# A gated mixer and ConvFFN step on one core: recurrence products moved from GpSimd to VectorE, one operand's low parts formed on VectorE, raw weight blocks of the gate pairs placed in other buffers

## The chip, the cores and the metric

The kernel runs on one NeuronCore of a Trainium2 chip. The metric is device time in microseconds of one execution, the median of several runs. Five engines matter here: TensorE (PE, the matmuls; PEld is its weight load), VectorE (DVE), ScalarE (ACT), GpSimd (POOL) and SyncE (SP), which here only issues DMA transfers. They run side by side and wait for one another through semaphores.

## The reference, cut to what matters

One layer is computed for 512 grid tokens of a denoising step and, with the same weights, for 128 context tokens; the kernel treats them as 640 columns. All is float32. In short:

```python
h = rmsnorm(x, norm1_g) * (1 + sc1) + sh1            # sc, sh, g from silu(c) @ w_ada + b_ada
proj = h @ w_in                                      # 13 sections
y_b = hgrn2_bidir(b_q, b_ff, b_fb, b_i, b_g, ...)    # recurrence, forward and backward
merged = sum_i sigmoid(h @ w_gate_i + b_i) * (y_i @ w_br_i)   # i = a, b, c, d
x = x + g1 * (merged @ w_o)
h = rmsnorm(x, norm2_g) * (1 + sc2) + sh2
x = x + g2 * conv_ffn(h, w_up, cw, cb, w_down)
```

The recurrence of a head is, with gates f = lb + (1 - lb) sigmoid(z), keys k = (1 - lb) sigmoid(-z) and decays that are products of f between two positions: `scores[t, s] = sum_d q[t, d] k[s, d] decay[t, s, d]`, `o = scores @ v` plus the part that comes from the carried state, once forward and once backward.

## The kernel before, in words

**Precision and products.** Each float32 matmul is made from three products of a high part (rounded to fp32r by a ScalarE copy) and a low part (the rest, by a VectorE subtraction): high x high, high x low, low x high. So each weight block costs a ScalarE copy and a VectorE subtraction (`feat`, L354 and L355, L367 and L368 in the `wsplit` and `prep` helpers), and each activation operand as well. In some places the subtraction is replaced by `low_dma`: ScalarE writes the negated high part, and a transfer issued by GpSimd adds the raw block onto it in SBUF.

**Order of the work.** The program is a list of units (a weight tile each): 26 projection tiles, 8 gate tiles of branch d, the gate pairs, 8 tiles of w_o, the up projection, 22 tiles of w_down. `ahead` loads the blocks of the next four units (SP) and splits those of the next two. Beside the units run generators (`hgrn`, `gmlp`, `conva`, `attn`, `ada_cols`, `norm2`), each of which yields the time after which it wants to go on, in microseconds of a planner's clock. `tick` and `pe` advance this clock by the estimated PE time of each matmul group, and `tick` starts the generators that are due; `drain` steps them all until a condition holds. This fixes the order in which instructions are written down. The framework then orders each engine's instructions itself, except those issued through `Ordered` (`ovec`, `oact`, `opool`) while `fixed[0]` is set, in the gate pairs and in the up pairs. [...]

**Recurrence** (`hgrn`). The state is not scanned; instead the scores are built in seven levels l = 0..6 with blocks of B = 2^l positions. At level l PE multiplies the queries `qq` with the keys of the neighbouring block (L559); VectorE or ScalarE puts the result into the score tile (L565, L569); then four multiplies in place (`ups`, L579) extend keys `kk` and queries `qq` by the gates `ff`, and L583 extends the gates. The matmul takes one tile of keys, half of whose columns are backward and half forward keys: `keys(l + 1)` builds it after the second multiply, half on GpSimd (L530), half on ScalarE (L531). Ahead of the levels come the sum `ksum` (L493), its product with the queries (L509), and the products of neighbours, one half on GpSimd and one on VectorE (L515, by the table `NE`). `along` sums over features by a matmul (L503). PE meanwhile works through the projection tiles; the section `i` is evacuated by ScalarE in L949.

**Gain columns** (`ada_cols`). 24 columns of w_ada are multiplied with silu(c) on VectorE (L256, two products per column) while the recurrence runs, 8 more (40 to 47) during the first half of w_down. Every eighth column of a gain ends with `gain_rows`, a PE transpose (L283), a ScalarE copy (L286) and a store.

**Gate pairs** (`g_pair`). Two gate tiles (n and n + 4 of a branch) are made with seven instead of eight block products. A pair has two raw blocks of 128x10x128; `gp_load` takes one from the pool `raw` (three buffers) and the other from `raw` too for even pairs, from the region `G` for odd ones. Pair 0 is loaded while the last branch-d gate tiles run (`gate_tile`, sigmoid L986); `g_a`, `g_sums`, `g_b`, `g_c` split blocks and their sums. The region G holds attention's values before the pairs and a part of x after them.

**Up projection** (`up_all`, `up_pair`). It uses the same seven products per pair, with seven activation operands made by `operands(c0, c1)`: x6 in region A, x5 in B, x7 in D; first for columns 0 to 192, then, when the last token tile is normalised, for 192 to 320. Their low parts: x6 by VectorE, x5 by transfer for the first columns and by VectorE for the last, x7 by transfer both times. For the first four pairs two of the seven products are made ahead (`up_start`), and the rest in 22 pairs. Much of this goes through `Ordered`, so the profile gives line L132 for it.

Of the kernel before, what the change touches and what calls it, by code (L numbers as in the profile page):

```python
# [9 lines left out]
F32 = mybir.dt.float32  # L10
# [3 lines left out]
ALU = mybir.AluOpType  # L14
AX = mybir.AxisListType

P = 128
HD = [4, 5, 2.1, 7, 2.2, 1.4, 1.5, 5, 2.0, 2, 11]
NE = [lambda p, v: p, lambda p, v: v]
OUTS = 1  # L20
NPAIR = 22
BRIDGE = 4
# [29 lines left out]
def tile_step(ctx: ExitStack, tc: tile.TileContext, a: dict, outs: list, dbg=None):  # L52
# [7 lines left out]
    rp = ctx.enter_context(tc.tile_pool(name="rp", bufs=3))  # L60
# [46 lines left out]
    def nm(s):  # L107
        cnt[0] += 1
        return f"{s}_{cnt[0]}"

    def region(tag, shape, dt=F32):
        return big.tile(shape, dt, tag=tag, name=nm(tag))
# [23 lines left out]
    ten, vec, pool, act, mm = nc.tensor, nc.vector, nc.gpsimd, nc.scalar.activation, nc.tensor.matmul  # L136
# [97 lines left out]
    def ada_cols(fs, tag, homes, gap):  # L234

        cr = region(tag, [P, 2, D])
        cf = cr.rearrange("p v c -> p (v c)")
        nc.sync.dma_start(cf, a["cc"].rearrange("v c -> (v c)").partition_broadcast(P))
        act(cf, cf, AF.Silu)
        raws = {}  # L240

        def load(f):
            if f in fs and f not in raws:
                raws[f] = homes(f)
                nc.sync.dma_start(raws[f], a["w_adt"][f - 16])

        load(fs[0])
        yield HD[4]
        for f in fs:
            load(f + 1)  # L250
            raw = raws.pop(f)
            junk = gp.tile([P, D], mybir.dt.bfloat16, tag="gt", name=nm("junk"))
            ar = sp.tile([P, 2], F32, tag="red", name=nm("ar"))
            for v in range(2):
                tc.keep_in_program_order(
                    vec.scalar_tensor_tensor(raw if v else junk, raw, 1.0, cr[:, v], ALU.mult, ALU.mult,  # L256
                                             accum_out=ar[:, v:v + 1]))
                yield HD[5]
            if f // 8 in (2, 5):
                vec.tensor_scalar(gcol[:, f // 8 // 5, :, f % 8], ar, p1[:, C_BADA + f:C_BADA + f + 1],  # L260
                                  None, ALU.add)
                if f % 8 == 7:
                    yield 2
                    gain_rows(f // 8 // 5)
            else:
                modulate(f, ar)
            yield gap
            while "hgrn_out" in R and "hgrn_done" not in R:
                yield 1
        R["ada%d" % fs[-1]] = True  # L270
# [213 lines left out]
    def hgrn():  # L484
        ff, kk, hd = R["FF"], R["KK"], R["HD"]
# [3 lines left out]
        sq = hd[:, 0:1280]  # L489
        ksum = hd[:, 1280:2560]  # L490
        vt = he[:, 1280:2560]
        f2 = lambda x: x.rearrange("p n t -> p (n t)")
        pool.tensor_tensor(ksum, f2(kk[:, 0]), f2(kk[:, 1]), ALU.add)  # L493
        vec.tensor_tensor(f2(qq[:, 0]), sq, f2(ff[:, 1]), ALU.mult)
        vec.tensor_tensor(f2(qq[:, 1]), sq, f2(ff[:, 0]), ALU.mult)
        yield 1
# [9 lines left out]
            return m  # L506


        pool.tensor_tensor(ksum, ksum, sq, ALU.mult)  # L509
        near = he[:, 0:1280]  # L510
        n2, q2 = near.rearrange("p (n j) -> p j n", j=2), lambda d: f2(qq[:, d]).rearrange("p (n j) -> p j n", j=2)
        k2 = lambda d: f2(kk[:, d]).rearrange("p (n j) -> p j n", j=2)
        yield HD[9]
        for j in range(2):
            NE[j](pool, vec).tensor_tensor(n2[:, j], k2(j)[:, j], q2(1 - j)[:, 1 - j], ALU.mult)  # L515
        dm = yield from along(ksum)

        near_at = hd[:, 1280:1920].rearrange("p (r i t) -> p r i t", r=2, i=10)
# [4 lines left out]
        def blk(x, B):  # L523
            return x.rearrange("p n t -> p (n t)").rearrange("p (n j i) -> p n j i", j=2, i=B)

        def keys(l):
            B = 1 << l
            kl = (he if l % 2 == 0 else hd)[:, 0:1280]
            klv = kl.rearrange("p (n j i) -> p n j i", j=2, i=B)
            pool.tensor_copy(klv[:, :, 0, :], blk(kk[:, 0], B)[:, :, 0, :])  # L530
            act(klv[:, :, 1, :], blk(kk[:, 1], B)[:, :, 1, :], AF.Copy)  # L531
            return kl

# [2 lines left out]
        for l in range(7):  # L536
            B = 1 << l
            e_, x_ = blk(kk[:, 0], B), blk(kk[:, 1], B)
            r_, p_ = blk(qq[:, 0], B), blk(qq[:, 1], B)
            f_, g_ = blk(ff[:, 0], B), blk(ff[:, 1], B)  # L540
            nb = 1280 // (2 * B)
            if l == 0:
                m = yield from along(near)
                vec.copy_predicated(nat, lmask[:, 0, :].unsqueeze(1).to_broadcast([P, 20, 32]), bc(m))

            W = 64 if l == 6 else 32
            ns = 320 // W
            for s0, par in ([(s_, r) for s_ in range(0, 10, ns) for r in range(2)] if l else ()):
                b = slice(64 * par, 64 * par + 64)
                m = pm()  # L550
                for i in range(s0, s0 + ns):
                    for g in range(P // W):
                        d, t0 = (0, W * g) if l < 5 else (1 - g % 2, W * (g ^ 1))
                        t0 += (i % 5) * P
                        rhs = qq[b, d, i // 5, t0:t0 + W]
                        if l < 5:
                            rhs = bass.AP(rhs.tensor, rhs.offset,
                                          [list(rhs.ap[0]), [2 * B, 16 // B], [1280 + B, 2], [1, B]])
                        mm(m[W * g:W * g + W, (i - s0) * W:(i - s0 + 1) * W],  # L559
                           kl[b, i * P + W * g:i * P + W * g + W], rhs,  # L560
                           start=True, stop=True, tile_position=(64 * par, W * g))
                    pe(0.18)
                mv = m[:, 0:ns * W].rearrange("p (i t) -> p i t", t=W)
                if l < 5:
                    vec.copy_predicated(near_at[:, par], lmask[:, l, :].unsqueeze(1).to_broadcast([P, 10, 32]), mv)  # L565
                else:
                    for g in range(P // W):
                        c = slice(W * g, W * g + W)
                        act(at[c, par, s0:s0 + ns, W * (g ^ 1):W * (g ^ 1) + W], mv[c], AF.Copy)  # L569
                if par == 0:  # L570
                    yield 0.4
            if l == 4:
                for g in range(4):
                    c = slice(32 * g, 32 * g + 32)
                    act(at[c, :, :, c].rearrange("p r i t -> p (r i) t"), nat[c], AF.Copy)
            ups = ((e_[:, :, 0, :], f_[:, :, 1, 0:1]), (x_[:, :, 1, :], g_[:, :, 0, 0:1]),
                   (p_[:, :, 1, :], f_[:, :, 0, 0:1]), (r_[:, :, 0, :], g_[:, :, 1, 0:1]))
            for i, (dst, mul) in enumerate(ups):
                vec.tensor_tensor(dst, dst, mul.to_broadcast([P, nb, B]), ALU.mult)  # L579
                if i == 1 and l < 6:  # L580
                    kl = keys(l + 1)
            fa = ff.rearrange("p d n t -> p (d n t)").rearrange("p (n j i) -> p n j i", j=2, i=B)
            vec.tensor_tensor(fa[:, :, 0, 0], fa[:, :, 0, 0], fa[:, :, 1, 0], ALU.mult)  # L583
            yield HD[1]
# [56 lines left out]
        for t in (4, 1, 2, 0, 3):  # L641
            m = pm()
# [23 lines left out]
        for t in range(5):  # L666
            m = pm()
# [396 lines left out]
    def gp_load(p_):  # L1064

        bi, n = gp_id(p_)
        r = [rp.tile([P, 10, P], F32, tag="raw", name=nm("raw"))]
        r.append(region("G", [P, 10, P]) if p_ % 2 else rp.tile([P, 10, P], F32, tag="raw", name=nm("raw")))
        for h in range(2):
            nc.sync.dma_start(r[h], a["w_gp"][GI[BR[bi]] * 4 + n, h])  # L1070
        return r
# [566 lines left out]
    def operands(c0, c1):  # L1638

        if "t" not in fx:  # L1640
            fx["t"] = region("X1", [P, 2, 4, HC])
            x6, x5, x7 = fx["xx"] = [region(t, [P, 2, 4, HC], F32R) for t in "ABD"]
            fx["x"].update({i: (x[:, 0], x[:, 1]) for i, x in ((6, x6), (5, x5), (7, x7), (4, hh[1]))})
        x6, x5, x7 = fx["xx"]
        t5, t6 = [fx["t"][:, i, :, c0:c1] for i in range(2)]
        a11, a12, a21, a22 = [hh[3 + i][:, j, :, c0:c1] for i in range(2) for j in range(2)]

        def split(w, x, dma=False):
            w = w[:, :, :, c0:c1]
            oact(w[:, 0], x, AF.Copy)  # L1650
            if dma:
                low_dma(w[:, 1], x)
            else:
                ovec.tensor_tensor(w[:, 1], x, w[:, 0].bitcast(F32), ALU.subtract)

        ovec.tensor_tensor(t5, a21, a22, ALU.subtract)
        ovec.tensor_tensor(t6, t5, a11, ALU.subtract)
        split(x6, t6)
        split(x5, t5, c0 == 0)
        ovec.tensor_tensor(a21, a11, a21, ALU.subtract)  # L1660
        split(x7, a21, True)
        ovec.tensor_tensor(t6, a12, t6, ALU.add)

    def operand3():
# [402 lines left out]
```

## Time and profile before

| | |
|---|---|
| time, median of 3 runs | 1064.63 us (1063.8 to 1064.79) |
| profiled execution | 1059.86 us |
| its span, first to last instruction | 1058.1 us |
| mean granted TensorE clock | 0.990 |
| busy: VectorE, ScalarE, GpSimd | 75%, 49%, 11% |

The stages by the timeline of the profiled execution: projections with recurrence, gMLP, convolution and attention from about 31 to 296 us, branch-d gate tiles to 369, gate pairs to 559, w_o to 616, up pairs to 890, w_down to the end. A row of the timeline gives start, duration, engine, line, operation, output<-inputs and, in brackets, how long the engine had been idle and what ended that. The view of waits gives the total, the number and the longest. The granted clock is 1.00 at full speed. Names of tiles come without their numbers; regions are named by their tag (A, B, D, G, X ...).

### The profile page before, as it was taken

To read this page: it belongs to the slowest core of one execution; us is meant where nothing else is said; L and a number is where in the kernel's file an instruction comes from. 1 tells how busy PE (TensorE), PEld (TensorE's weight loads), DVE (VectorE), ACT (ScalarE), POOL (GpSimd) and SP (SyncE) were. 2 spreads that over 40 slices of the span, in tenths; PEclk is the share of its full clock that TensorE was granted. 3 is DMA by queue.
4 is the path that set the end of the run, shared out by engine and by line. 5 is a ranking of instruction groups with operands and counts; after the bars stand their busy time and mean duration, and the time that the engine had idled before them with its cause. 6 is when DMAs were issued, how large, how long until landed. Compare 5 with 4: busy or idle time off the path is not lost.

```text
span 1058.1 us, 18808 instructions
## 1 busy us (share of the span) xinstructions
PE 1030.5 (97%) x7648; PEld 967.0 (91%) x7648; DVE 793.1 (75%) x1275; ACT 520.2 (49%) x893; POOL 119.4 (11%) x150
## 2 busy tenths in 40 slices
PE   8998999999999999999999998999999999999997
PEld 6798988998899999999998897999999999888886
DVE  6548799779956376676768686998888887695734
ACT  6352235333343244444545375777777677533532
POOL 1012023111100000000010021212211111000201
PEclk9998999999999999999999998999999999999999
DMA  9662534435134132422258485765666667984212
GB/s 374 230 244 67 173 103 141 146 116 169 59 116 150 50 101 75 150 75 76 90 176 327 174 254 105 197 163 145 154 160 163 169 154 219 363 279 160 80 41 100
DMA packets 53911, 166.33 MB, mean 157 GB/s; under 512 B 7840, under 2 KB 15936, under 8 KB 50752
## 3 DMA queue, kind: packets, MB, share of 16 engines
q1 hardware_dynamic: 42992, 137.19, 37.6%
q0 software_dynamic: 10832, 27.93, 11.5%
q8 instruction: 60, 0.98, 0.4%
q14 instruction: 27, 0.22, 0.1%
HBM read 131.52 MB, written 21.52 MB: 145 GB/s over the span
## 4 chain that ended last, share of the span: by engine, by line
PE 88%; DVE 3%; DMA 3%; issue 3%; ACT 1%; POOL 1%; SPq 0%; POOLq 0%; ACTq 0%; DVEq 0%
PE g L1474 20%; PE g L402 17%; PE m L1133 14%; PE g L1787 8%; PE m L1787 6%; PE m L1474 5%; PE g L1146 4%; PE m L1269 3%; PE g L1269 2%; PE g L945 1%; PE g L1889 1%; PE m L212 1%; DMA ycd<-C 1%; PE m L885 1%; DMA D<-X 1%
## 5 line engine op out<-in xcount | busy, mean ns | idle before, releaser
L402 PE MATMUL g<-XH,w 128*128 128x320 f32 x832 | 198.7, 316 | 2.4 <-ACT gt L986 2.4
L402 PEld LDWEIGHTS g<-XH,w 128*128 128x128 f32 x832 | 141.6, 188 | 4.8 <-ACT gt L986 2.6
L402 PE MATMUL g<-XL,w 128*128 128x320 f32 x416 | 128.8, 310 | 0.0
L402 PEld LDWEIGHTS g<-XL,w 128*128 128x128 f32 x416 | 78.3, 188 | 0.4 <-issue 0.2
L355 DVE TENSOR_TENSOR w<-raw,w 128x1024 fp32r<-128x1024 f32 x34 | 41.5, 1221 | 21.1 <-ACT w L354 20.4
L1787 PE MATMUL g<-w,XH 128*128 128x512 f32 (+1 forms) x216 | 47.5, 372 | 0.0
L1787 PEld LDWEIGHTS g<-w,XH 128*128 128x128 f32 x216 | 38.5, 188 | 7.3 <-DVE X L132 0.2
L368 DVE TENSOR_TENSOR w<-raw,w 128x1024 fp32r<-128x1024 f32 (+1 forms) x29 | 41.3, 1423 | 5.2 <-ACT w L367 5.1
L1133 PE MATMUL m<-XH,w 128*128 128x320 f32 x192 | 45.0, 309 | 0.0
L354 ACT ACTIVATE w<-raw 128x1024 fp32r<-128x1024 f32 x34 | 35.8, 1052 | 18.6 <-PE g L1269 10.2
L367 ACT ACTIVATE w<-raw 128x1024 fp32r<-128x1024 f32 (+1 forms) x29 | 32.5, 1119 | 19.4 <-PE g L402 11.7
L132 DVE SCALAR_TENSOR_TENSOR X<-MG,p2t,X 128x641 f32<-128x641 f32 x44 | 38.9, 884 | 3.5 <-ACT X L132 2.6
L1787 PE MATMUL m<-w,XH 128*128 128x512 f32 (+1 forms) x180 | 40.3, 368 | 0.0
L1787 PE MATMUL g<-w,XL 128*128 128x512 f32 (+1 forms) x180 | 40.1, 373 | 0.0
L132 DVE SCALAR_TENSOR_TENSOR X<-X,p2t,X 128x641 f32<-128x641 f32 x44 | 38.9, 884 | 1.2 <-ACT X L132 0.3
L1474 PE MATMUL g<-XL,C 128*128 128x320 f32 x240 | 38.6, 310 | 0.4 <-ACT MG L132 0.4
L1474 PE MATMUL g<-XL,w 128*128 128x320 f32 x240 | 38.7, 310 | 0.0
L1787 PEld LDWEIGHTS g<-w,XL 128*128 128x128 f32 x180 | 32.2, 188 | 6.8 <-DVE dt L1798 0.6
L1474 PEld LDWEIGHTS g<-XL,C 128*128 128x128 f32 x240 | 36.0, 188 | 1.1 <-ACT MG L132 1.1
L1474 PEld LDWEIGHTS g<-XL,w 128*128 128x128 f32 x240 | 35.9, 188 | 0.7 <-ACT MG L132 0.3
L1787 PEld LDWEIGHTS m<-w,XH 128*128 128x128 f32 x180 | 31.3, 189 | 5.3
L1787 PE MATMUL m<-w,XL 128*128 128x512 f32 (+1 forms) x150 | 33.2, 368 | 0.0
(542 smaller groups left out, 2727.1 us busy)
## 6 DMA issues: line engine op xcount, KB each, us to landing
raw<-in_w_up_dram SPq DMA_DIRECT2D x31, 512.0 KB, 5.0
raw<-in_w_gp_dram SPq DMA_DIRECT2D x18, 640.0 KB, 3.9
raw<-in_w_in_dram SPq DMA_DIRECT2D x22, 512.0 KB, 4.1
raw<-in_w_down_dram SPq DMA_DIRECT2D x22, 512.0 KB, 4.0
H<-in_w_adt_dram SPq DMA_DIRECT2D x16, 512.0 KB, 3.5
actd<-X POOLq DMA_DIRECT2D x22, 320.5 KB, 5.3
X<-in_w_adt_dram SPq DMA_DIRECT2D x11, 512.0 KB, 3.6
G<-in_w_up_dram SPq DMA_DIRECT2D x11, 512.0 KB, 4.5
```

The lines of the kernel that those rows point to most:

```text
L132: r = f(*args, **kw)
L212: mm(m[32 * g:32 * g + 32, 0:256], scv[:, k, :], raw[:, k, :], start=(k < 4), stop=(k >= 4), tile_position=(0, 32 * g))
L354: act(w[0], raw, AF.Copy)
L355: vec.tensor_tensor(w[1], raw, w[0].bitcast(F32), ALU.subtract)
L367: act(w[:, 0], raw, AF.Copy)
L368: low = lambda: vec.tensor_tensor(w[:, 1], raw, w[:, 0].bitcast(F32), ALU.subtract)
L402: mm(o, w[:, h, k0 + k, :], r(k)[:, s], start=(k == 0 and i == 0), stop=(k == kt - 1 and i == 2))
L1133: mm(o, w[:, k, :], x[:, k, :], start=(first and k == 0 and j == 0), stop=(k == 3 and j == 2), skip_group_check=True)
L1146: mm(pb[:, c, 0:HC], w[:, h + k, :], y[:, x, k, s], start=(k == 0 and j == 0), stop=(k == 1 and j == 2))
L1269: mm(m, mh[k // 2][:, hx, k % 2, t * P:(t + 1) * P], wo[q][:, hw, k % 2, :], start=(k == 0 and i == 0), stop=(k == 7 and i == 2))
L1474: mm(o, w[:, k, :], x[:, k, :], start=(first and k == 0 and j == 0), stop=(k == 3 and j == 2), skip_group_check=True)
L1787: mm(acc[nh][t + c0 // 256][:, 0:c1 - c0], sl[k][hx][:, t * P:(t + 1) * P], w[:, hw, k, c0:c1], start=(kk_ == 0 and k == 0 and i == 0), st ...
```

## The change

Five edits:

1. In the recurrence `ksum`, its product with the queries, both halves of the neighbours' products and the key copy of L530 go from GpSimd to VectorE; the table `NE` goes.
2. `keys` is built for levels 1 to 4 only. Levels 5 and 6 give PE the keys straight from `kk`: in these levels a group of W positions is all backward or all forward, so no mixed tile is needed.
3. `ada_cols` yields 10 instead of 2 planner microseconds between the last column of a gain and its transpose; all later columns move by as much.
4. `gp_load` uses region G for even pairs and two raw buffers for odd ones.
5. `operands` makes x7's low part by a VectorE subtraction in both calls instead of by transfer.

```diff
-NE = [lambda p, v: p, lambda p, v: v]
...
                 if f % 8 == 7:
-                    yield 2
+                    yield 10
                     gain_rows(f // 8 // 5)
...
-        pool.tensor_tensor(ksum, f2(kk[:, 0]), f2(kk[:, 1]), ALU.add)
+        vec.tensor_tensor(ksum, f2(kk[:, 0]), f2(kk[:, 1]), ALU.add)
...
-        pool.tensor_tensor(ksum, ksum, sq, ALU.mult)
+        vec.tensor_tensor(ksum, ksum, sq, ALU.mult)
...
-            NE[j](pool, vec).tensor_tensor(n2[:, j], k2(j)[:, j], q2(1 - j)[:, 1 - j], ALU.mult)
+            vec.tensor_tensor(n2[:, j], k2(j)[:, j], q2(1 - j)[:, 1 - j], ALU.mult)
...
-            pool.tensor_copy(klv[:, :, 0, :], blk(kk[:, 0], B)[:, :, 0, :])
+            vec.tensor_copy(klv[:, :, 0, :], blk(kk[:, 0], B)[:, :, 0, :])
...
+                        k0 = i * P + W * g
                         rhs = qq[b, d, i // 5, t0:t0 + W]
                         if l < 5:
+                            lhs = kl[b, k0:k0 + W]
                             rhs = bass.AP(rhs.tensor, rhs.offset,
                                           [list(rhs.ap[0]), [2 * B, 16 // B], [1280 + B, 2], [1, B]])
-                        mm(m[W * g:W * g + W, (i - s0) * W:(i - s0 + 1) * W],
-                           kl[b, i * P + W * g:i * P + W * g + W], rhs,
+                        else:
+                            lhs = f2(kk[:, g % 2])[b, k0:k0 + W]
+                        mm(m[W * g:W * g + W, (i - s0) * W:(i - s0 + 1) * W], lhs, rhs,
                            start=True, stop=True, tile_position=(64 * par, W * g))
...
-                if i == 1 and l < 6:
+                if i == 1 and l < 4:
                     kl = keys(l + 1)
...
-        r.append(region("G", [P, 10, P]) if p_ % 2 else rp.tile([P, 10, P], F32, tag="raw", name=nm("raw")))
+        r.append(region("G", [P, 10, P]) if p_ % 2 == 0 else rp.tile([P, 10, P], F32, tag="raw", name=nm("raw")))
...
-        split(x7, a21, True)
+        split(x7, a21)
```

## The prediction

> **What bounds the kernel now.** I read the page's part 1 first, then the view of what TensorE waited for (us in total, times, longest), then the windows with their granted clock, and last the timelines around each wait. First the page:
>
> ```profile
> span 1058.1 us, 18808 instructions
> ...
> PE 1030.5 (97%) x7648; PEld 967.0 (91%) x7648; DVE 793.1 (75%) x1275; ACT 520.2 (49%) x893; POOL 119.4 (11%) x150
> ```
>
> TensorE (PE) is busy for 97% of its span; 27.6 us are idle. The profiled execution took 1059.86 us, 1.76 more than the span, and the median of the three runs is 1064.63, 4.77 above that. The trace doesn't say where these 4.77 lie. I work out the difference on the trace and subtract it from the median. With PE this full, an edit is worth what it takes from PE's idle time or gives back of its clock, and nothing else. So, what did PE wait for?
>
> ```profile
> PE g L1474 <- DMA D<-X: 4.2, 1, 4.2
> PE g L945 <- ACT E L949: 3.1, 1, 3.1
> ...
> PE g L402 <- ACT gt L986: 2.4, 1, 2.4
> ...
> PE m L283 <- DVE gcol L260: 0.8, 1, 0.8
> ```
>
> These are four single waits, one in each place that the diff touches: the seventh operand's transfer, the recurrence, the last gate tile before the pairs, and the transpose of the gain column. Together 10.45 us. Two of them cost more than their length. Windows (PE busy with its matmul count, ..., clock, DMA share, GB/s), the pairs for line L945 and for line L1474 alone:
>
> ```profile
> 80.00:84.00 4.00, 4.00 (x36) 4.00 (x35) 1.00 0.01 4
> 93.00:97.00 4.00, 3.92 (x18) 3.69 (x18) 0.50 0.18 45
> ...
> 642.00:647.00 5.00, 5.00 (x20) 5.00 (x20) 0.50 0.02 3
> 652.00:657.00 5.00, 5.00 (x36) 5.00 (x35) 1.00 0.48 162
> ...
> 98.00:99.00 1.00, 1.00 (x9) 1.00 (x10) 0.58 (x1) 0.29 (x1) 0.00 (x0) 0.95 0.06 25
> ...
> 647.00:648.00 1.00, 1.00 (x7) 1.00 (x6) 1.00 (x3) 0.48 (x1) 0.83 (x2) 0.67 0.00 0
> ...
> 340.00:350.00 10.00, 7.77 (x53) 7.77 (x54) 4.97 (x7) 2.69 (x4) 0.00 (x0) 1.00 0.19 69
> ```
>
> After the wait that ends at 92.81 PE runs at half clock, 18 matmuls in 4 us where 36 went before, until 98.05 (the window 98 to 99 has a mean clock of 0.95): 5.2 us at half pace, **2.6 us lost**. After the one that ends at 641.66 it runs 20 matmuls in 5 us where 36 go later, until about 647.3: 5.7 x (1 - 20/36) = **2.5 us lost**. The wait of 2.4 us near 340 is followed by no such stretch (clock 1.00).
>
> [...]
>
> **Recurrence.** The chain behind the second wait (start, duration, engine, line; in brackets the idle time before and its releaser):
>
> ```profile
> 79.84 1.49 DVE L494 TENSOR_TENSOR C<-D,A 128x1280 f32<-128x1280 f32 x1 [4.87 <-ACT D L446]
> 79.95 4.19 POOL L509 TENSOR_TENSOR D<-D 128x1280 f32<-128x1280 f32 x1 [9.91 <-ACT D L446]
> 81.25 3.97 DVE L368 TENSOR_TENSOR w<-raw,w 128x1024 fp32r<-128x1024 f32 x1
> ...
> 86.76 2.31 POOL L515 TENSOR_TENSOR E<-B,C 128x640 f32<-128x640 f32 x1 [2.62 <-PE m L945]
> 89.10 1.56 DVE L579 TENSOR_TENSOR B<-B,A 128x640 f32<-128x640 f32 x2 [1.74 <-POOL E L515]
> ...
> 90.76 0.81 ACT L531 ACTIVATE D<-B 128x640 f32<-128x640 f32 x1 [10.00 <-DVE B L579]
> ...
> 92.40 0.36 ACT L949 ACTIVATE E<-g 128x256 f32<-128x256 f32 x1
> 92.81 0.58 PE L945 MATMUL g<-w,XH 128*128 128x256 f32 x1 [3.08 <-ACT E L949]
> 94.01 1.21 DVE L368 TENSOR_TENSOR w<-raw,w 128x1024 fp32r<-128x1024 f32 x1
> ```
>
> While GpSimd forms L509 (4.19 us), VectorE's L368 takes 3.97 us; the same instruction takes 1.21 at 94.01, so 2.76 are lost. Then VectorE idles 1.74 us for GpSimd's half of L515. Only then come the two L579 multiplies, for which ScalarE's key copy L531 has waited; the evacuation L949 is queued behind it, and PE, idle since 89.73, needs L949. With everything on VectorE, in the same order: L494 1.49, L368 1.21, L495 and L509 1.49 each (L494's shape), L515 two halves and L579 two multiplies at 0.78 each (1.56 for two) = 8.8 us from 79.84; successive instructions overlap by about 0.08, so 8.2 to 8.8. The multiplies end at 88.1 to 88.6 instead of 90.66, 2.0 to 2.6 us sooner, and L949 at 90.2 to 90.8. PE still waits 0.5 to 1.1; I take 0.7. Gain 3.1 - 0.7 + 2.6 (no half clock after so short a wait) = **5.0 us**; bounds 2.0 (the half clock stays) and 5.7.
>
> [...]
>
> The other moves, with their rows:
>
> ```profile
> 57.67 0.55 DVE L443 TENSOR_SCALAR B<-B,lbt 128x640 f32<-128x640 f32 x1
> ...
> 73.75 1.23 DVE L355 TENSOR_TENSOR w<-raw,w 128x1024 fp32r<-128x1024 f32 x1 [6.83 <-ACT w L354]
> ...
> 99.16 1.22 DVE L256 SCALAR_TENSOR_TENSOR H<-H,S 128x1024 f32<-128x1024 f32 x1
> ...
> 130.00:205.00 75.00, 72.23 (x1183) 67.28 (x1182) 70.15 (x146) 33.21 (x73) 13.99 (x10) 1.00 0.39 129
> ...
> 159.38 1.55 DVE L579 TENSOR_TENSOR B<-B,A 128x640 f32<-128x640 f32 x2
> ...
> 160.76 0.82 PE m L559 x58
> ...
> 167.82 0.90 DVE L579 TENSOR_TENSOR B<-B,A 128x640 f32<-128x640 f32 x1
> ...
> 170.78 0.73 PE m L559 x20
> ```
>
> L493 (1.49) falls into VectorE's idle 6.83 us before 73.75: free. The four key copies left go to VectorE. Before shows no VectorE copy of that size; a one-input instruction over 128x640 took 0.55 (L443), a two-input one 0.78, so 2.2 to 3.1 in all; a copy has one input, I take 2.2. They stand behind the multiplies that free ScalarE, so they delay only VectorE's own queue. From 130 to 205 VectorE is busy for 70.15 of 75 us, and PE takes its results there; added in that stretch are two copies (1.1 to 1.6), and against it goes what `yield 10` pushes out: 8 us of the planner, in which a column takes 5.0 (1.4 + 1.4 + 2.2), so one and a half columns of two 1.22 us products (L256), 3.7 us. Cost: nothing, covered by those.
>
> Levels 5 and 6 now read `kk` directly, so VectorE's multiply of `kk` must wait until PE has read it. That is a new wait. At level 5 PE's matmuls end at 161.58 and the multiply started at 159.38: 2.2 us; at level 6 171.51 against 167.82: 3.7 us. Behind the multiply stand L368 (the next tile's low weights) and the products L256, which need neither. From 0 (the framework puts those in front) to 5.9 us of VectorE time; PE feels it only beyond the 4.85 us of VectorE's idle time and the 3.7 just freed. I take 0. ScalarE's two copies and GpSimd's two simply go.
>
> **Gain column.** `yield 10` puts the transpose L283 8 us of the planner behind its column; the wait of **0.8 us** goes, bounds 0 and 0.8. The row it makes is loaded only for w_o, hundreds of microseconds later.
>
> **Gate pairs.** SP's queue, VectorE and ScalarE before the third wait:
>
> ```profile
> 329.38 17.09 SPq L1070 DMA_DIRECT2D raw<-in_w_gp_dram  x3
> ...
> 335.62 1.48 DVE L368 TENSOR_TENSOR w<-raw,w 128x1280 fp32r<-128x1280 f32 x1
> ...
> 341.08 0.42 ACT L132 ACTIVATE H<-raw 128x256 fp32r<-128x256 f32 x1 [8.66 <-DMA raw<-in_w_gp_dram]
> 341.40 0.78 ACT L986 ACTIVATE gt<-g,p1t 128x640 f32<-128x640 f32 x1
> ```
>
> The second raw block of pair 0 shares a buffer with the tile whose split L368 ends at 337.10; its load has landed when ScalarE's copy starts, at 341.08. That copy (`H<-raw`) has waited 8.66 us for it, the sigmoid L986 (`gt`) is queued behind, ends at 342.18, and PE restarts. In region G, which attention left long before, the block can be loaded right behind the first one (329.38), some 4 us of transfer each: it is there by about 337.5 even if the two follow one another, and with the copy (0.42) and the sigmoid (0.78) behind it `gt` is done by 338.7. PE ran dry only at 339.8 (342.2 less 2.4). The wait of **2.4 us** goes; bounds 0 and 2.4. Pair 1 then needs two raw buffers, but its second is the one its first used before, so it starts no later. At the other end the last odd pair now holds two raw buffers, so w_o's second and third block get theirs one pair later in SP's queue; PE reads them only after the last pair. Cost 0, covered by that pair; at most 2.4, what a late raw block costs here.
>
> **Seventh operand.** Forms of 626 to 641 us (count, busy, mean ns), and the rows around the first wait:
>
> ```profile
> L132 DVE TENSOR_TENSOR A<-X,A 128x768 fp32r<-128x768 f32 x1 | 1.0, 952 | 0.0
> ...
> L132 DVE TENSOR_TENSOR A<-X,A 128x512 fp32r<-128x512 f32 x1 | 0.7, 693 | 0.0
> ...
> 634.08 1.29 POOL L132 DMA_DIRECT2D D<-X  x1 [1.22 <-ACT D L132]
> 641.66 0.60 PE L1474 MATMUL g<-D,E 128*128 128x320 f32 x1 [4.18 <-DMA D<-X]
> 645.44 0.56 DVE L132 TENSOR_TENSOR X<-g,X 128x192 f32<-128x192 f32 x2 [5.72 <-ACT X L132]
> ```
>
> The second accumulating transfer of `D` starts at 634.08, PE is idle from 637.48 and goes on when it has landed, at 641.66. In its place come two VectorE subtractions, 0.95 + 0.69 = 1.64 us, while ScalarE loses two copies and GpSimd two transfers to issue. VectorE is full there until 639.7, then idle for 5.72 us; so all 1.64 may reach PE, as the low parts of the sixth operand or of the next weights come later. Gain 4.2 + 2.5 - 1.6 = **5.1 us**; bounds 1.5 and 6.7. Is VectorE late next?
>
> ```profile
> 662.57:674.89 12.32, 12.32 (x85) 12.07 (x84) 12.11 (x19) 9.37 (x17) 2.27 (x3) 1.00 0.83 200
> ```
>
> In the pair after next it is busy for 12.11 of 12.32 us with PE unbroken. It would lag 1.6 us more; PE held through 12.11 before, but little room is left. That is the second rival.
>
> **Sum.** 5.0 + 0.8 + 2.4 + 5.1 = 13.3. The framework lays most engines' orders anew, so I leave 0.7 for small new waits of the size it has now: 12.6 less, **1052.0 us**; the profiled execution would take about 1047.3.
>
> **Rivals.** 1. The recurrence wait stays: VectorE is late for another reason. Against it, 3.97 beside 1.21 exactly under L509. Then 0.8 + 2.4 + 5.1 = 8.3 less: 1056.3. Chance 0.14.
> 2. VectorE takes the transfer's place in the first up pairs and gives back what the clock gained: 1.5 instead of 5.1, 9.7 in all, so 1054.9. For it, 12.11 of 12.32; against, 5.72 us of idle before 645.44. Chance 0.12.
> 3. The gate blocks don't do what they should, because SP holds the G load behind another wait: 10.9 instead of 13.3, so 1053.7. Chance 0.04.
> 4. More gain: the 4.77 us between the profile and the timed runs are about two half-clock stretches of 2.5; if one follows the 2.4 us wait in those runs, where the trace shows none, it goes too. That is 2.5 to 4.8 beside the 13.3: about 1048. [...] Chance 0.10.
> 5. Slower: VectorE becomes the recurrence's bound. The new waits at levels 5 and 6 (5.9), the products and copies (1.5 + 0.8 + 3.1) add 11.3 us; PE's waits there are short now only because VectorE is just on time. If none is covered, the 5.8 gained in recurrence and column are lost, and 11.3 appear on PE: 1064.6 - 7.5 + 11.3 = 1068.4. It decides from 7.5 us of late VectorE on. Against it, idle 4.85 us, 3.7 pushed out, 4.5 of blocked and idle time removed. Chance 0.07.
> 6. New waits elsewhere in the re-laid orders eat it all: 1064. Chance 0.03.
>
> **How the numbers follow.** Forecast 0.50 at 1052.0, its own range 1049 to 1055. The whole range, 1046.5 to 1061, takes in rivals 1 to 4 and the unknown costs, and leaves out 5, 6 and the edges. By 0.2% (2.1 us, about what a measurement of this kernel can tell from no change): faster 0.88, same 0.05, slower 0.07.
>
> **What would show it.** Right: PE's waits for `E` L949 and `D` are under 1.5 us each, no window at 0.50 near 95 or 645, no wait for `gt`, none for `gcol`; L368 near 82 takes 1.2; VectorE's busy share of 130 to 205 is no higher. Wrong: a PE wait for VectorE above 3 us with a half clock behind it, near 160 to 190 or 640 to 700.

## The result, and the profile after

The changed kernel took 1050.64 us (median of 4 runs, 1047.71 to 1051.51) beside 1064.71 (4 runs of the kernel before, 1063.8 to 1069.24): a ratio of 0.9855, 95% interval 0.9821 to 0.9889. In a second comparison, with more runs, it took 1049.92 beside 1061.52, ratio 0.9901 (0.9872 to 0.9929). The forecast was 1052.0, or 12.6 us less; over the 90 runs of before that were taken beside the experiments and all 10 runs of after the medians are 1062.5 and 1050.1, 12.4 apart. The profiled execution took 1051.51 us.

First the page of the changed kernel (busy time, share, instructions), then the view of PE's waits (total, times, longest):

```profile
span 1049.7 us, 18767 instructions
...
PE 1030.0 (98%) x7648; PEld 967.4 (92%) x7648; DVE 795.3 (76%) x1284; ACT 518.7 (49%) x889; POOL 95.6 (9%) x139
```

```profile
PE g L1891 <- ACT XH L1853: 2.6, 2, 1.5
PE g L1476 <- ACT X L131: 1.5, 1, 1.5
PE m L562 <- issue: 1.5, 1, 1.5
...
PE g L1476 <- DMA B<-X: 1.0, 1, 1.0
PE g L1476 <- ACT MG L131: 1.0, 2, 0.5
PE g L1476 <- DVE A L131: 0.4, 1, 0.4
```

PE's idle time fell from 27.6 to 19.7 us. The four waits of the prediction (D 4.2, E 3.1, gt 2.4, gcol 0.8) are gone; ahead of the seventh operand's product stand three short ones: A 0.4 and MG 0.5 (of the 1.0), as before, and B 1.0, which is new. The longest entries left were there before, except `X` (1.5) and `B`.

**Recurrence.** The timeline of VectorE and ScalarE at the place of the old wait:

```profile
79.99 1.49 DVE L493 TENSOR_TENSOR C<-D,A 128x1280 f32<-128x1280 f32 x1 [4.87 <-ACT D L445]
81.40 1.22 DVE L367 TENSOR_TENSOR w<-raw,w 128x1024 fp32r<-128x1024 f32 x1
...
83.93 1.49 DVE L508 TENSOR_TENSOR D<-D 128x1280 f32<-128x1280 f32 x1
85.34 1.56 DVE L514 TENSOR_TENSOR E<-B,C 128x640 f32<-128x640 f32 x2
86.81 1.56 DVE L581 TENSOR_TENSOR B<-B,A 128x640 f32<-128x640 f32 x2
88.94 0.39 ACT L951 ACTIVATE E<-g 128x256 f32<-128x256 f32 x1 [0.82 <-PE g L947]
89.23 0.79 ACT L530 ACTIVATE D<-B 128x640 f32<-128x640 f32 x1
```

L367 (L368 before) takes 1.22 instead of 3.97 us, the multiplies end at 88.37 (forecast 88.1 to 88.6), and ScalarE now evacuates L951 before the key copy L530 instead of behind it. PE doesn't wait at all. VectorE is not fuller in the stage that was in doubt: it is busy for 65.47 of 75 us there, 70.15 before:

```profile
130.00:205.00 75.00, 73.48 (x1035) 69.58 (x1035) 65.47 (x134) 31.01 (x67) 6.79 (x8) 0.98 0.38 119
```

**Gate pairs and seventh operand.** ScalarE's sigmoid for `gt`, 6.6 us earlier and now released by PE, no longer queued behind the copy of the raw block; then PE's three waits, the transfer that the third waits for, one of the two new subtractions, and VectorE's idle time behind them (5.72 before):

```profile
334.77 0.80 ACT L988 ACTIVATE gt<-g,p1t 128x640 f32<-128x640 f32 x1 [5.72 <-PE g L401]
...
626.76 1.88 PE L1476 MATMUL g<-A,E 128*128 128x320 f32 x11 [0.42 <-DVE A L131]
629.17 0.41 PE L1476 MATMUL g<-B,E 128*128 128x320 f32 x1 [0.53 <-ACT MG L131]
630.57 2.27 PE L1476 MATMUL g<-B,E 128*128 128x320 f32 x11 [0.99 <-DMA B<-X]
624.13 1.33 POOL L131 DMA_DIRECT2D B<-X  x1 [4.99 <-ACT B L131]
624.76 0.95 DVE L131 TENSOR_TENSOR D<-X,D 128x768 fp32r<-128x768 f32 x1
...
636.22 0.56 DVE L131 TENSOR_TENSOR X<-g,X 128x192 f32<-128x192 f32 x2 [1.55 <-ACT X L131]
```

`D` is there in time. The transfer of `B`, the fifth operand, was issued 5.04 us before PE's first matmul with `B`, about as long ahead as before (5.19); PE went on 6.4 us after the issue here and 6.7 in the second profile of after. So it lands on the edge: PE's wait for it is none in both profiles of before, 0.5 in that of the recurrence alone, 1.0 and 1.2 in the two of after, 0.6 without the gate blocks and none in the kernel of experiment 10.

**Where the time came from.** First and last start of two groups that both kernels have in the same order (count, shortest/median/longest ns, first and last start), before and after, the first in the gate pairs, the second in the up pairs:

```profile
L1133 PE MATMUL m<-XH,w x192: 309/309/309, 368.7 to 541.1; 128*128 128x320 f32 x192
...
L1474 PE MATMUL m<-XH,w x108: 309/309/309, 687.6 to 886.4; 128*128 128x320 f32 x108
```

```profile
L1135 PE MATMUL m<-XH,w x192: 309/309/309, 362.7 to 535.1; 128*128 128x320 f32 x192
...
L1476 PE MATMUL m<-XH,w x108: 309/309/309, 677.1 to 875.9; 128*128 128x320 f32 x108
```

The lead is 6.0 us through all gate pairs and 10.5 through all up pairs after the first ones: 4.5 come from the seventh operand, 6.0 from what lies ahead (recurrence, gain column, gate block, and a loss near 147, below). The up pairs keep their pace of 12.32 us. Of the 10.5 the spans show 8.4, mostly because of the one wait of 1.52 us for `X` at 884.59. It stands in none of the other profiles of this study: ScalarE, which copies `X`, had been held for 1.67 us by the transfer of `E<-actd` that its queue's next copy needed.

**What had not been forecast** is a half clock in two new places. In the windows (PE busy, ..., clock, DMA share, GB/s) each stretch of 3.41 us is cut where the clock changes:

```profile
143.68:147.09 3.41, 1.89 (x122) 1.54 (x108) 2.74 (x7) 0.27 (x1) 0.00 (x0) 1.00 0.27 59
147.09:150.50 3.41, 3.41 (x20) 3.38 (x14) 3.25 (x6) 2.67 (x4) 0.00 (x0) 0.50 0.28 107
...
624.95:628.37 3.42, 3.00 (x21) 2.73 (x19) 3.42 (x6) 1.39 (x3) 0.51 (x1) 1.00 0.90 149
628.37:631.78 3.41, 1.90 (x11) 1.44 (x11) 3.41 (x7) 3.23 (x5) 0.30 (x7) 1.00 0.10 16
631.78:635.19 3.41, 3.41 (x15) 3.41 (x14) 2.88 (x3) 0.16 (x1) 0.00 (x0) 0.50 0.53 151
635.19:638.61 3.42, 3.42 (x25) 3.42 (x24) 2.36 (x5) 2.52 (x5) 0.94 (x2) 1.00 0.01 2
```

Before 147.09 there is one wait of 1.5 us (in the profile of before the same kind, 1.6 us, left the clock at 1.00), before 631.78 two of the three short ones, 0.53 and 0.99, in one window; the first, 0.42, ends at 626.76, in the window before. PE is busy throughout the two stretches at 0.50, so each costs up to 1.7 us, half its length.

### The profile page after: what moved, and what is told of

It reads as the page before. It is cut to its first block, busy times and chain, and to the rows that moved or that the text cites. A ratio compares the mean times of both kernels' runs of the same rounds, so it can differ in the third digit from the quotient of the medians.

```text
span 1049.7 us, 18767 instructions
## 1 busy us (share of the span) xinstructions
PE 1030.0 (98%) x7648; PEld 967.4 (92%) x7648; DVE 795.3 (76%) x1284; ACT 518.7 (49%) x889; POOL 95.6 (9%) x139
## 4 chain that ended last, share of the span: by engine, by line
PE 92%; DVE 2%; DMA 2%; issue 2%; ACT 1%; POOL 0%; SPq 0%; POOLq 0%; ACTq 0%; DVEq 0%
PE g L1476 19%; PE g L401 19%; PE m L1135 14%; PE g L1789 8%; PE m L1789 6%; PE m L1476 5%; PE g L1148 4%; PE m L1271 3%; PE g L947 2%; PE g L1271 2%; PE g L1891 1%; PE m L562 1%; PE m L211 1%; PE m L887 1%; DMA E<-actd 1%
## 5 line engine op out<-in xcount | busy, mean ns | idle before, releaser
L401 PE MATMUL g<-XH,w 128*128 128x320 f32 x832 | 201.2, 318 | 0.2 <-DVE MG L462 0.2
L367 DVE TENSOR_TENSOR w<-raw,w 128x1024 fp32r<-128x1024 f32 (+1 forms) x29 | 37.5, 1294 | 5.7 <-ACT w L366 5.5
```

The costliest lines, as they stand in the source:

```text
L367: low = lambda: vec.tensor_tensor(w[:, 1], raw, w[:, 0].bitcast(F32), ALU.subtract)
L401: mm(o, w[:, h, k0 + k, :], r(k)[:, s], start=(k == 0 and i == 0), stop=(k == kt - 1 and i == 2))
```

## The experiments

All kernels below are the kernel before or the changed one with one edit. Beside the median I give two means worked out from each run's span and mean granted clock: **time at full clock** (span x clock) and **time lost to the clock** (span x (1 - clock)). The clock is given to 0.001, so one run's value is good to 0.5 us; the means of 5 to 90 runs have standard errors of 0.1 to 0.4 at full clock and of 0.4 to 0.9 in the loss. The two aren't quite independent: idle time inside a half-clock stretch counts half in the first, and in the 90 runs of before the first falls by 0.19 us for each us of loss.

| kernel | runs | median us | ratio to before, 95% | at full clock | lost to clock |
|---|---|---|---|---|---|
| before (beside the experiments, and 1.) | 90 | 1062.5 | | 1047.3 | 13.2 |
| after (both comparisons) | 10 | 1050.1 | 0.9855 / 0.9901, above | 1041.6 | 7.2 |
| recurrence alone | 12 | 1056.72 | 0.9950 (0.9933 to 0.9967) | 1046.1 | 9.0 |
| seventh operand alone | 10 | 1057.57 | 0.9954 (0.9932 to 0.9977) | 1044.0 | 11.2 |
| gate blocks alone | 24 | 1062.6 | 1.0004 (0.9988 to 1.0021), 1.0001 (0.9978 to 1.0023) | 1045.3 | 15.2 |
| after without gate blocks | 6 | 1052.57 | 0.9909 (0.9882 to 0.9936) | 1043.4 | 7.4 |
| after, x5 on VectorE too | 5 | 1048.35 | 0.9879 (0.9856 to 0.9902) | 1041.9 | 4.8 |
| after, less of the recurrence | 6 | 1048.82 | 0.9874 (0.9844 to 0.9904) | 1041.1 | 5.9 |
| before, filled wait | 12 | 1062.43 | 0.9994 (0.9969 to 1.0018) | 1048.3 | 11.9 |

**1. The kernel before, again** (no edit).

> The kernel before, run several times for the granted clock of each run. Its profiled execution took 1059.86 us at a mean clock of 0.990, its timed runs 1063.8 to 1064.8. Theory A (the 4.8 us between them are half-clock stretches whose presence depends on how the waits fall into the clock's window): the runs near 1064 show a clock of 0.987 to 0.988, those near 1060 show 0.990, and us against clock lies on a line of about 1.05 us per 0.001. Theory B (something else, transfers or the start): the clock stays at 0.990 whatever the time.

Theory A held. The 12 runs lie between 1056.03 us at a clock of 0.994 and 1067.8 at 0.983: 11.8 us for 0.011. Span times clock was 1047.4 in the median of these runs, with a standard deviation of 1.4. (Over all 90 runs the line is flatter than expected, 0.86 us for 0.001.) The profile, of a run with a span of 1066.0, has the same waits as the first profile of before at the places of the diff, but the stretch behind the wait for E is three windows long instead of two:

```profile
94.67:98.08 3.41, 1.14 (x11) 0.94 (x9) 2.90 (x4) 1.24 (x2) 1.77 (x2) 1.00 0.00 0
98.08:101.50 3.42, 2.61 (x12) 2.61 (x13) 3.42 (x4) 0.76 (x2) 0.00 (x0) 0.50 0.00 0
101.50:104.91 3.41, 3.41 (x18) 3.41 (x18) 1.22 (x3) 0.77 (x2) 0.00 (x0) 0.50 0.49 154
104.91:108.32 3.41, 3.41 (x18) 3.41 (x18) 3.41 (x6) 0.07 (x1) 0.00 (x0) 0.50 0.18 42
108.32:111.74 3.42, 3.42 (x26) 3.42 (x26) 1.35 (x3) 1.65 (x3) 0.00 (x0) 1.00 0.28 111
```

These cuts are not chosen for this place. **In each of the 14 profiles of this study all changes of the clock between 13 and 1035 us lie on one lattice with a pitch of 3.413 us**: in the first profile of before the half clock begins at 23.0, 91.3 and 640.85, that is 20 and 161 pitches apart; here at 16.15, 26.4, 36.65, 98.1, 350.65 and 651.05. Where the lattice lies differs from one execution to the next (its remainder in 3.413 is 2.5 in these two, 0.3 in the profile of after, 2.9 in that of the recurrence alone, 0.1 in that of the seventh operand alone). So by these profiles a run's time is what the waits leave plus up to 1.7 us for every window at half clock, and which waits get one depends on where they fall.

**2. Recurrence alone.**

```diff
-        pool.tensor_tensor(ksum, f2(kk[:, 0]), f2(kk[:, 1]), ALU.add)
+        vec.tensor_tensor(ksum, f2(kk[:, 0]), f2(kk[:, 1]), ALU.add)
...
-                if i == 1 and l < 6:
+                if i == 1 and l < 4:
```

(and the other lines of edits 1 and 2.)

> Only the recurrence's edits (products and copies on VectorE, no key copies for levels 5 and 6). Theory: PE's wait for E (3.1) and the half clock behind it (2.6) go, 5.0 to 5.7 less than before: about 1059. Rival 1 (VectorE late for another reason): no gain, 1064.7. Rival 5 (VectorE becomes the bound at levels 5 and 6): 1068. If only the wait goes and the half clock turns up at another place (the profile after has one of 3.4 us near 147): 3.1 + 2.6 - 1.7 = 4.0 less, 1060.7.

5.6 us less in the median, 0.5% (0.33 to 0.67). The wait is gone from the profile, and so is the half clock behind it; there is none near 147 in that execution. It is the clock that gains most, 4.2 us; at full clock only 1.2 are gained. Of the wait's 3.1 us, 0.6 to 1.8 lay in half-clock windows already, in the seven profiles that have it, and count half there. And in this profile PE waits longer further on, for `gt` (2.4 and 1.9 in the two of before) and for `D` (4.2 and 4.4):

```profile
PE g L1477 <- DMA D<-X: 4.8, 1, 4.8
PE g L402 <- ACT gt L989: 3.0, 1, 3.0
```

So by this one profile 1.0 to 1.7 us of the recurrence's gain are lost again further on; why isn't shown. (Without the gate blocks, in experiment 6, the wait for `gt` is as long, 3.1.) Rivals 1 and 5 are out.

**3. Only the product L509.**

```diff
-        pool.tensor_tensor(ksum, ksum, sq, ALU.mult)
+        vec.tensor_tensor(ksum, ksum, sq, ALU.mult)
```

> Only the product of keys and queries (L509) and its sum (L493) on VectorE; the neighbours' half L515 and the key copies stay on GpSimd. Theory (GpSimd's L509 and VectorE's L368 exclude each other): L368 near 81 takes 1.2 instead of 3.97. If that alone is what makes the multiplies late, they end 1.3 us sooner and PE's wait for E falls to about 1.8; if GpSimd's L515 (2.31) binds as well, VectorE still waits 1.5 or more for it and PE's wait for E stays above 1.5. Rival 1 (L368 is slow for another reason): 3.97 stays, PE's wait at 3.1 or more.

The kernel that ran moves the product alone; the sum L493, which the expectation counts in, stayed on GpSimd, as its row shows. One run (1054.72 us, clock 0.994). The rows at the same place, and PE's wait:

```profile
81.47 1.22 DVE L368 TENSOR_TENSOR w<-raw,w 128x1024 fp32r<-128x1024 f32 x1
...
85.41 2.48 DVE L515 TENSOR_TENSOR E<-B,C 128x640 f32<-128x640 f32 x1
87.82 1.55 DVE L579 TENSOR_TENSOR B<-B,A 128x640 f32<-128x640 f32 x2
67.29 2.98 POOL L493 TENSOR_TENSOR D<-B 128x1280 f32<-128x1280 f32 x1 [30.67 <-DVE B L443]
84.23 2.99 POOL L515 TENSOR_TENSOR E<-B,C 128x640 f32<-128x640 f32 x1 [13.97 <-issue]
90.17 0.37 ACT L949 ACTIVATE E<-g 128x256 f32<-128x256 f32 x1
```

```profile
PE g L945 <- ACT E L949: 0.2, 1, 0.2
```

L368 takes 1.22 instead of 3.97 as soon as GpSimd is quiet: rival 1 falls, GpSimd's L509 was the cause. The stretching moves to the next pair that still runs side by side: VectorE's half of L515, 0.78 when both run on VectorE, takes 2.48 and ends 0.67 us after GpSimd's half (84.23 + 2.99 = 87.22 against 87.89). Before, L368 had ended 1.08 us after L509 (85.22 against 84.14). Each time VectorE's instruction ends about its own length after GpSimd's (1.08 for one of 1.22, 0.67 for one of 0.78), as if it had waited for the whole of it; these two pairs are all that the runs show of it. (GpSimd paid too: L509, which began beside VectorE's L494, took 4.19, and L493, of the same size with VectorE idle, 2.98.) The second half of this expectation missed: GpSimd's L515 still costs VectorE 1.7 us, and yet PE waits for 0.2 us only. The multiplies end at 89.37, 1.3 sooner, and ScalarE's weight copy L367, which stood between the key copy and L949, has moved ahead of both, another 1 us.

**4. Seventh operand alone.**

```diff
-        split(x7, a21, True)
+        split(x7, a21)
```

> Only the seventh operand's low parts on VectorE. By the prediction 5.1 less (1059.6). By the profile after, which still has three waits of 0.42, 0.53 and 0.99 us there and 3.3 us at half clock: 4.2 + 2.5 - 1.6 - 1.7 = 3.4 less, about 1061.3. Rival 2 (VectorE gives it back in the up pairs): 1.5 or less, 1063.2.

4.7 us less, 0.46% (0.23 to 0.68): between the two estimates. In its profile the wait for `D` (4.2) is gone, there is no half clock near 640, and PE's new wait is 0.9 for `w` (the next low weights, released by VectorE, probably late by its added work). 3.3 us at full clock, 2.0 of the clock. Rival 2 is out: VectorE gives back 0.9, not 3.6.

**5. and 6. Gate blocks alone, and the changed kernel without them.**

```diff
-        r.append(region("G", [P, 10, P]) if p_ % 2 else rp.tile([P, 10, P], F32, tag="raw", name=nm("raw")))
+        r.append(region("G", [P, 10, P]) if p_ % 2 == 0 else rp.tile([P, 10, P], F32, tag="raw", name=nm("raw")))
```

> Only the raw blocks of the gate pairs placed anew. Theory: the wait of 2.4 us for gt goes and nothing comes in its place: 1062.3. Rival 4 (in the timed runs a half-clock stretch stands behind that wait, which the profile of before does not show): 2.4 + 2.5 = 4.9 less or a little more, 1059.8. Rival 3 (the load is held up elsewhere): 1064.7.

> Only the raw blocks of the gate pairs placed anew, a second time. In its first 12 runs the wait for gt was gone and span times clock 2.1 below that of before, yet the median was that of before, at a mean clock of 0.9856 against 0.9878. Theory (how many half-clock windows a run gets at its other waits depends on where the lattice of windows falls, and those 12 runs got one more by chance): the median is 2.0 to 3.7 below that of the kernel before, span times clock again near 1045.4, the mean clock at or above that of before. Rival (the edit itself costs clock, for instance by making the wait for D longer): the median again that of before and the mean clock again lower by 0.002.

> The changed kernel with the gate pairs' raw blocks placed as before. Theory: PE waits for gt again, 1.4 to 2.4 us, and in a good part of the runs a half-clock window follows (1.7): span times clock 2.0 more than the changed kernel, the median 2.0 to 3.7 more: 1052 to 1053.7. Rival (from the run of this edit alone, which showed no gain in its median): no difference, 1050.

Alone the edit gains nothing that the median shows, in 24 runs, though the wait for `gt` is gone from both profiles. At full clock it gains 2.0 us (2.1 and 1.5 against the runs of before beside each half), and the clock loses 2.0 more. I had taken the first twelve runs for chance; the second twelve are the same, so the rival held, though not by the longer wait for `D` that it offered (4.6 and 4.4 in these profiles, 4.2 and 4.4 before). Why these runs have more half-clock windows stays open: the two profiles have theirs at 31, 92 and 642 us, and at 15, 32, 94, 149, 159 and 643, all ahead of or far behind the edit. In the changed kernel the edit is worth 1.8 us at full clock and 0.2 of the clock; the medians, 2.5 apart, and their overlapping intervals alone would not show it. Without it the wait comes back. PE's wait in this profile; then the windows at this place in the first profile of before, with no half clock behind the wait; then those of this profile, with two half-clock windows:

```profile
PE g L401 <- ACT gt L988: 3.1, 1, 3.1
```

```profile
340.46:343.87 3.41, 1.64 (x11) 1.64 (x12) 2.72 (x5) 2.26 (x3) 0.00 (x0) 1.00 0.01 3
343.87:347.28 3.41, 3.41 (x25) 3.41 (x24) 2.25 (x3) 0.00 (x0) 0.00 (x0) 1.00 0.05 12
```

```profile
334.07:337.48 3.41, 1.34 (x10) 1.07 (x8) 0.09 (x1) 0.16 (x1) 0.00 (x0) 1.00 0.59 192
337.48:340.90 3.42, 2.43 (x9) 2.43 (x10) 3.42 (x7) 2.10 (x3) 0.00 (x0) 0.50 0.00 0
```

**7. Gain column alone.**

```diff
-                    yield 2
+                    yield 10
```

> Only the later transpose of the gain column. Theory: PE's wait of 0.8 to 1.0 for gcol goes, all other waits stay (E 3.1, D 4.2 to 4.4, gt 1.7 to 2.4). Rival: the columns that come later cost as much at another place, shown as a new wait on DVE in 130 to 205.

One run (1062.74 us): the wait for `gcol` is gone, no wait for VectorE has come in its place, the others stay (E 3.1, D 4.3, gt 1.4).

**8. The changed kernel again** (no edit).

> The changed kernel once more, for its times on the same chip as the other runs and for the granted clock of more of its runs. If a run's time is a fixed part plus 1.71 us for each window of 3.41 us at half clock (as the profiles so far lie on such a lattice): span times clock within 1 us of 1042 in every run, the clock between 0.991 and 0.996, the median near 1050.5. If the first four runs were lucky in their clock: up to 1054.

1049.92 (6 runs, 1048.82 to 1056.09), clock 0.995 to 0.988, span times clock between 1040.8 and 1041.9. One run at 0.988 shows that this kernel too can meet a bad lattice, below the bounds I gave; 1040.8 lies 0.2 below the other bound.

**9. Fifth operand on VectorE too.**

```diff
-        split(x5, t5, c0 == 0)
+        split(x5, t5)
```

> The changed kernel with the fifth operand's low parts formed on VectorE for the first columns as well, so that no transfer is left in these operands. Theory (PE's wait of 0.99 for B is the transfer, and the three waits of 0.42, 0.53 and 0.99 together starve the window before the half clock at 631.8): the 0.99 goes, VectorE's 0.95 is covered by its idle 1.55 behind, the half-clock window goes in the phases that had it: 1.0 to 2.7 less than the changed kernel, about 1048.5. Rival (VectorE is already the bound there): its 0.95 delays A and D, a wait of about 1 us stays, same time.

1048.35 beside 1049.92; the intervals overlap, so no gain is shown. The wait for `B` is gone, but others have come, in this order 1.5 us for the copy of `A` on ScalarE and 0.7 for its subtraction:

```profile
PE g L1476 <- ACT A L131: 1.5, 1, 1.5
...
PE g L1476 <- DVE A L131: 0.7, 1, 0.7
```

So the rival was right about the waits: VectorE's added work comes back as waits for `A`. At full clock it is the same (1041.9, 1041.6). What it may gain is the clock: its profile has no half-clock window at this place or near 147. But that isn't shown to come from the edit, as two windows here have about as little PE work (1.91 and 2.16 us) as the one (1.90) that brought the half clock in after:

```profile
623.34:626.75 3.41, 1.91 (x12) 1.44 (x10) 3.41 (x6) 0.63 (x1) 0.00 (x0) 1.00 0.23 91
626.75:630.17 3.42, 2.16 (x14) 1.89 (x14) 3.35 (x7) 1.39 (x3) 0.29 (x7) 1.00 0.02 5
```

**10. Less of the recurrence's edit.**

```diff
-            vec.tensor_tensor(n2[:, j], k2(j)[:, j], q2(1 - j)[:, 1 - j], ALU.mult)
+            NE[j](pool, vec).tensor_tensor(n2[:, j], k2(j)[:, j], q2(1 - j)[:, 1 - j], ALU.mult)
...
-            vec.tensor_copy(klv[:, :, 0, :], blk(kk[:, 0], B)[:, :, 0, :])
+            pool.tensor_copy(klv[:, :, 0, :], blk(kk[:, 0], B)[:, :, 0, :])
...
-                if i == 1 and l < 4:
+                if i == 1 and l < 6:
```

> The changed kernel with less of the recurrence's edit: only ksum and its product with the queries on VectorE; the neighbours' half, the key copies and the copied keys of levels 5 and 6 stay as before. Theory (the product L509 alone held up VectorE): PE's wait for E is 0.2 and the time that of the changed kernel, 1050, within 1. Rival (the remaining GpSimd work stretches VectorE's instructions enough to show later): 1 to 3 more, with PE waits for VectorE in 85 to 205.

1048.82 us, ratio 0.9874; no slower than the changed kernel, and by intervals not faster either. PE's wait for E is 0.2. So L493 and L509 carry all that the recurrence's edit gains, and by experiment 3, where PE's wait for E was 0.2 with L493 still on GpSimd, L509 alone may; the other half of the edit is worth nothing that can be measured.

**11. A filled wait.**

```diff
             prod(b2, p_, 5, True)
+            if p_ == 0:
+                for k in range(36):
+                    mm(up[0, "g"][:, 1, HC:512], up[0, "B"][:, 0, k % 4, :], fx["x"][5][0][:, 0, 0:192],
+                       start=True, stop=True, skip_group_check=True)
             prod(b1, p_, 7, False)
```

> The kernel before, with 36 matmuls of 192 columns put in front of the seventh operand's product; their result (in unused columns of that PSUM tile) is used by nothing. They keep PE busy for some 3.5 us of the 4.2 to 4.6 in which it waits for D, and take no time from other work. Theory (a window of 3.41 us in which PE is busy for less than about 0.6 puts the next at half clock): the wait as such stays, but the two half-clock windows behind it (642 to 649 in the runs of before, 3.4 us lost) go: 2.5 to 3.4 less than before, about 1059, and a mean clock higher by 0.003. Rival (the half clock comes from something else there, transfers or ScalarE): the stretch stays, time as before, 1062.

Against the expectation the 36 matmuls change a result: one output of this kernel is off by 0.19 of its size. How isn't shown, and only the kernel's time is read here. PE in the first up pair:

```profile
638.12 4.16 PE L1639 MATMUL g<-B,E 128*128 128x192 f32 x36
...
642.65 0.38 PE L1474 MATMUL g<-D,E 128*128 128x320 f32 x1 [0.21 <-DMA D<-X]
...
643.02 0.45 PE L1474 MATMUL g<-D,E 128*128 128x320 f32 x2
```

The matmuls fill the wait, and the rows behind run at full pace (0.45 us for two instead of 0.73): no half clock near 640 in this profile, as the theory has it. (Its 0.6 was my estimate: of the windows at full clock in the 14 profiles with PE busy for less than 0.6, 30 of 36 were followed by one at half clock.) But the time missed its forecast: 0.06% less, with an interval from -0.31 to +0.18%. The clock gave 1.3 us back instead of 2.5 to 3.4, and 1.0 is lost at full clock, part of it because idle time at half clock counts half. The profile supports the cause; the time neither shows the gain nor excludes 2.5.

## Why the forecast was right, and where it was not

**Recurrence, 5.0 (2.0 to 5.7).** Right, with its mechanism: L368 at 1.2, multiplies at 88.37, and 5.6 less (3.5 to 7.1) from this edit alone. Two terms were off. The residual wait of 0.7 is 0, because ScalarE's order changed, which the prediction had kept as it was; in experiment 3 that is worth about 1 us. (The 90.2 to 90.8 given for L949 is by its rows PE's restart, 0.4 later.) And the half clock, put at 2.6 from one profile, costs more on average: in the seven profiles that have this wait, 1 to 3 windows follow it (17 in all), by PE's busy time in them 3.6 us a profile. That nothing is lost at levels 5 and 6 held: VectorE waits there for PE for 0.5 us once, against the bound of 5.9.

**Gain column, 0.8.** The wait went, in the changed kernel and alone. Its time was not measured by itself.

**Gate pairs, 2.4 (0 to 2.4).** 1.5 to 2.1 at full clock; the mechanism is right. That it shows in the time at all was taken for granted, and alone it doesn't.

**Seventh operand, 5.1 (1.5 to 6.7).** 4.5 in the profile, 4.7 (2.4 to 7.2) alone: right in sum. The cost of 1.6 on VectorE was the term that was off: here it costs PE nothing (alone 0.9, for `w`), and VectorE, in the up pairs as full as before, holds nobody up. In its place PE waits 1.0 for `B`'s transfer, which had no term, and gets a half-clock window again. The half clock behind `D` was read to end at 647.3; it ended at 647.65, which adds 0.2 to the 2.5. The lower bound, 1.5, has no working: with the clock's 2.5 gone, 2.6 would be left.

**No half clock after so short a wait.** This step failed. The prediction took each wait by itself, with some length between 2.4 and 3.1 us from which the clock drops; no run shows such a length. The profiles speak for a window instead: by the tally in the last section a half clock followed all 15 windows of 3.41 us in which PE was busy for less than 0.45 and 24 of the 34 from 0.45 to 0.65, in whichever waits the idle time lay. Two waits of 0.53 and 0.99 in one window did it at 631.78, and a single one of 1.5 at 147.09. (The expectations of experiments 4 and 9 count the wait of 0.42 in; it lies in the window before.) So "no window at 0.50 near 645" came out wrong, as this work runs near 632 now. In the profiled execution there are three half-clock windows ahead of the end instead of five: two windows fewer are 3.4 us, not the 5.1 of the sum. Over all runs the loss to the clock is 6.0 us smaller (13.2 against 7.2), and of the sum's 7.5 us from the waits 5.7 show at full clock. The old windows behind E cost more than the sum had and the new ones took something back; how the 6.0 come about in full isn't shown. That 12.6 met 12.4 so well is in part luck.

**The small new waits, 0.7.** Beside `B` (1.0 and 1.2) the profiles of after have hardly any: 1.5 us for `X` in one of the two, none in the other.

**Rival 4** (more gain, from the 4.77 us between the profile of before and its timed runs) was right about the nature of these 4.77 as far as the record goes: 2.6 of them are half-clock windows of which the first profile happened to have few (a loss of 10.6 us to the clock, against 13.2 in the mean of 90 runs). But the changed kernel has its own, so they don't come as a gain on top. The forecast's other figure, 1047.3 for the profiled execution, missed by 4.2, mostly for this reason and the 1.5 for `X`: the two profiles differ by 8.4 us, not by 12.6. The 14.07 of the first comparison, with 4 runs on each side, is more than the 12.4 of all runs, probably for the same reason: a few runs are a small sample of lattices.

## What to carry to other kernels

A VectorE instruction that is slow in one place only was explained here by what ran beside it (L368, 3.97 us beside GpSimd's L509 and 1.22 without): look for a GpSimd instruction that ends just before, and move that one; the other GpSimd work could stay (1048.82 us with it on GpSimd, 1050.1 without). A PE that waits for one transfer shows what the next one is worth only when the first is gone: look how closely the others land. And where a profiled execution differs from the timed runs, compare span times granted clock as well as the time: in the 90 runs of before its standard deviation was 1.1 us, that of the time 2.9.

## What the runs showed of the hardware

**Windows at half clock followed windows with little PE work.** In 14 profiles, between 13 and 1035 us, I cut PE's time at the lattice of 3.413 us. Of the windows at full clock in which PE was busy for less than 0.45, all 15 were followed by a window at half clock; from 0.45 to 0.65, 24 of 34; from 0.65 to 0.75, 3 of 34, all three full of 64x32 matmuls; above that none. So the busy share doesn't decide alone: three of the ten that were not followed are quoted above (1.64 of 3.41 us at 340.46, and the two of experiment 9). Of 16 windows at half clock with PE busy for less than 0.9, 13 were followed by another; of 49 fuller ones 4, with PE busy throughout and all at one place, the second window behind the wait for `E` (101.50 above). What decides there is open.

**The spread of a measurement goes with the clock.** The kernel before took 1055.4 to 1068.23 us in 90 runs, 1.2%, with the same instructions, and a standard deviation of 2.9 us; that of span times clock was 1.1. The edit of the gate blocks, 2.0 us at full clock in 24 runs, so vanished in the median (5 and 6).
